# State product of the scan with C as the stationary operand, and the sample's sub-key scores in full-width matmuls

## The chip, the cores and the metric

The kernel runs on one core of a Trainium2 chip. A core has a matrix engine (TensorE, PE in the profile, its weight loads PEld), a vector engine (VectorE, DVE), a scalar engine (ScalarE, ACT), GpSimd (POOL) and SyncE (SP), which only issues transfers; ACT and POOL issue transfers too. Sixteen DMA engines serve them all. Each engine works through its own list of instructions in order and waits for others by semaphores.

The metric is the device time of one launch in microseconds.

## The reference, cut to what matters

One step of a decoder layer for a prompt of 256 tokens and a sample of 8 sequences of 8 tokens each (64 tokens), all in float32, with a model width of 2048: a mixer (a state-space scan, SSD, beside a short convolution), attention over 256 memory tokens, and PEER, which picks 16 experts out of 16384 for each of 8 heads by two sets of 128 sub-keys. The change touches two places. In the scan, for each sequence b, head r of group g and token l:

```python
cb = jnp.einsum('bclgn,bcsgn->bgcls', cc, bc)
y_diag = jnp.einsum('bgcls,bgrcls,bcsgrp->bclgrp', cb, lmat, xdt)
...
y_off = jnp.einsum('bclgn,bcgrpn,bgrcl->bclgrp', cc, new_states[:, :-1], jnp.exp(a_cs))
y = (y_diag + y_off)...
```

For the sample, `new_states[:, :-1]` is the state that comes in from memory (8 sequences, 32 heads, 64 channels a head, 128 state elements). `y_off` is thus, per sequence, the product of 8 rows of C (8 tokens x 128) with the state of each head (64 x 128), scaled by the decay `exp(a_cs)` of head and token. Four groups of 8 heads share one C each.

In PEER the query of a token and head, two halves of 128, is multiplied with the two sets of sub-keys:

```python
q = (xt @ wq).reshape(T, PEER_HEADS, 2, PEER_HALF)
s = jnp.einsum('thid,hikd->thik', q, sub_keys).astype(f32)
s1, i1 = lax.top_k(s[:, :, 0], K)
```

## The kernel before, in words

Activations lie with their 2048 features on 16 blocks of 128 partitions and the 320 tokens along the free axis: columns 0 to 255 are the prompt (`TP` = 256), 256 to 319 the sample (`TS` = 64, `NB` = 8 sequences of `LS` = 8 tokens).

The backbone is a stream of projections. Weights come in tiles W through SyncE's queue into four rooms of half a megabyte (`wtile`). Each half of a tile is split into a high and a low part in a reduced float32 format: ScalarE makes H (line 248), VectorE makes L = W - H (line 249), seven buffers each (`HLB`). TensorE then does three matmuls for each block, of the high and low parts of weight and activation (lines 367 to 369, 320 columns), 12 for a unit of work. The class `Stream` writes the program: weights are loaded `WA` = 3 tiles ahead, splits are made up to `GD` = 6 units ahead of the matmuls, and `pop` emits one unit's matmuls. After each pop, `Stream` advances a list of side generators by a rate each, and these emit everything else: the scan, the attention's softmax, the sub-key scores, the top-16 searches. So the order on TensorE, ScalarE and VectorE is the order in which the program is written; GpSimd's order in these stages is set by a scheduler when the kernel is built. A steady generator also issues, from ScalarE's queue, copies of expert rows from memory to memory (`u_d`), 0.272 of a copy per pop.

The scan (`ssd`, `group`) is a side generator with a rate of 0.7 (`R_SSD`) and runs beside the projections of the scan's inputs and of the short convolution. For each of the four groups g it prepares products of B and C (`ptcb`, line 789 and on), inputs by token (`XD`, `XQ`), and then goes through four chunks j of 128 channels (two heads each). Per chunk: GpSimd has loaded the states of the 8 sequences (`SB`, 128 x 8 x 128, two buffers); TensorE transposes them (`pst`, line 241) and ScalarE copies them to `ST` (line 880), so that the state axis lies on the partitions; then TensorE does the state product `YO` (line 887): for each sequence its `ST` block, 128x128, is stationary and the 8 columns of C are streamed. VectorE multiplies `YO` by the decays `EE` into `YE` (line 888). TensorE forms the new states (`pns`, line 891), VectorE updates `SB` and GpSimd stores it. At the end of a chunk come the within-chunk products `py` (line 913), two heads in two halves of 64 columns of the array, and VectorE adds `py` and then `YE` to `XS` (lines 914 and 915).

In PEER, eight panels of the query projection run through the same stream. `evac_p` multiplies the result by the token norms into q (line 1566, VectorE), two tiles of 128 x 320 a panel. The side generator `scores` multiplies q with the sub-keys `KY`: for the prompt four matmuls (`psc`, line 1578), 128 tokens each; for the sample `pscs` (line 1585), 64 tokens, done twice so that the scores stand on both halves of the 128 partitions. ScalarE copies both to `SS` (lines 1580 and 1586), and VectorE searches them for the top 16 (`best_keys`, lines 1593 to 1601), in the same in-order list as the splits L and the q of later panels. Beside this, `normed` (line 1536 and on) sends the normed input through memory into the tile `XP`.

All matmuls named here other than the projections and pns are in full float32, which the profile records as two passes each.

Of the kernel before, what the change touches and what calls it, by code (L numbers as in the profile page):

```python
# [11 lines left out]
F32 = mybir.dt.float32  # L12
# [151 lines left out]
def step(ctx, tc, ins, outs, dbg=None, stop=None):  # L164
# [417 lines left out]
    strm.then(pMs.close)  # L582


    pS = pSs = DTT = AT = DN = AN = ACN = DD = ACS = EE = BC = REP = DR = MB = None

    def open_s():
        nonlocal pS, pSs, DTT, AT, DN, AN, ACN, DD, ACS, EE, BC, REP, DR, MB
        pS, pSs = pool("pS")
        DTT = pS.tile([NH, T], F32, name="DTT")  # L590
        AT = pS.tile([NH, T], F32, name="AT")
        DN = pS.tile([P, 3, NH], F32, name="DN")
        AN = pS.tile([P, 3, NH], F32, name="AN")
        ACN = pS.tile([P, 3, NH], F32, name="ACN")
        DD = pS.tile([P, 3, NH], F32, name="DD")
        ACS = pS.tile([NH, T], F32, name="ACS")
        EE = pS.tile([P, KC, TS], F32, name="EE")
        BC = pS.tile([P, 8, T], F32, name="BC")

        REP = pS.tile([TS, 2, P], F32, name="REP")  # L600
        S.activation(REP.rearrange("p q (r t) -> p q r t", r=4),
                     ident[0:TS, 0:TS].rearrange("p (q t) -> p q t", q=2).unsqueeze(2).broadcast_to([TS, 2, 4, 32]), AF.Copy)
        DR = pS.tile([P, 2, NH], F32, name="DR")
        MB = pS.tile([P, 4], F32, name="MB")

    strm.then(open_s)

# [138 lines left out]
    def group(g):  # L746
# [42 lines left out]
        PE.matmul(pt[:, 0:TP], Bc[:, 0:P], Cc[:, 0:TP], start=True, stop=True)  # L789
        PE.matmul(pt[:, TP:TP + P], Bc[:, P:TP], Cc[:, P:TP], start=True, stop=True)  # L790
        PE.matmul(pt[0:TS, 384:448], Bc[:, TP:T], Cc[:, TP:T], start=True, stop=True)
        CM = pS.tile([P, 448], F32, tag="CM", bufs=1, name="CM")
        V.tensor_tensor(CM[:, 0:P], pt[:, 0:P], TRI, ALU.mult)
        S.activation(CM[:, P:TP], pt[:, P:TP], AF.Copy)
# [67 lines left out]
            V.tensor_tensor(LM, LM, CM[:, 0:384], ALU.mult)  # L862
            lms.append(LM)

        YE = pS.tile([P, 4, TS], F32, tag="YE", bufs=1, name="YE")
        for j in range(4):
            c = 4 * g + j

# [3 lines left out]
            if j == 0:  # L872
                bcast(1)
            yield 1
            ST = pS.tile([P, NB, P], F32, tag="ST", bufs=1, name="ST")
            for q in range(2):
                pt = ps("pst")
                for b in range(4):
# [3 lines left out]
            yield 1  # L882
            lmat(2 * j + 1)
            yield 1
            YO = ps("YO")
            for b in range(NB):
                PE.matmul(YO[:, LS * b:LS * b + LS], ST[:, b], Cc[:, TP + LS * b:TP + LS * b + LS], start=True, stop=True)
            V.tensor_tensor(YE[:, j], YO[:, 0:TS], EE[:, c], ALU.mult)
            for q in range(2):
                pt = ps("pns")  # L890
                PE.matmul(pt, XQ[:, q, j * P:(j + 1) * P], BD[:, q].rearrange("p b n -> p (b n)"), start=True, stop=True)
# [19 lines left out]
            for pair in zip(*parts):  # L911
                for o, w, m, first, last in pair:
                    PE.matmul(o, w, m, start=first, stop=last)
            V.scalar_tensor_tensor(XS[:, c], XS[:, c], DC[:, c:c + 1], py[:, 0:T], ALU.mult, ALU.add)
            V.tensor_tensor(XS[:, c, TP:T], XS[:, c, TP:T], YE[:, j], ALU.add)
            yield 1

    def mark(*what):
# [643 lines left out]
    def evac_p(m, pt, c):  # L1562
        if m == 0:
            PP["q"] = []
        q = PP["pool"].tile([P, T], F32, tag="q", bufs=2, name="q")
        V.tensor_tensor(q, pt[:, 0:T], RS["p"], ALU.mult)
        PP["q"].append(q)
        if m == 1:
            strm.side(scores(c, PP["q"]), 1)

    def scores(c, qs):
# [9 lines left out]
        yield 1  # L1581
        pt = ps("pscs")
        for j, q in enumerate(qs):
            for r in range(2):
                PE.matmul(pt[TS * r:TS * r + TS, j * P:(j + 1) * P], q[:, TP:T], PP["KY"][:, 2 * c + j], start=True, stop=True)
        S.activation(PP["SS"][:, 2, 2 * c + 1:2 * c + 3], pt[:, 0:2 * P].rearrange("p (j k) -> p j k", k=P), AF.Copy)
        done.add(("score", c))
        yield 1
# [606 lines left out]
```

## Time and profile before

| | before |
|---|---|
| median of 3 runs | 3156.19 us (3151.37 to 3171.6) |
| profiled execution, its own time | 3160.18 us |
| its span, first to last instruction | 3158.5 us |
| TensorE busy | 3091.9 us, 98% |
| weight loads busy | 2829.5 us, 90% |
| VectorE, ScalarE, GpSimd busy | 2277.1, 1597.2, 1306.5 us |
| granted TensorE clock, mean | 0.992 |

The span is what the profile covers; 1.7 us of the profiled execution lie outside it. Busy time of a matmul is from its start to its modelled end, so matmuls that follow each other overlap and the sum of their durations is more than the time they take; the chain of waits shows instead how far each one pushes the next one's start. The scan lies between about 340 and 820 us from the span's start, the sub-key scores between 1530 and 1660. A row of a tile or line has the engine, the operation, what it writes and reads, its count, its shortest, median and longest duration in ns, and the first and last start.

### The profile page before, as it was taken

The numbers are of one execution on the slowest core, as the hardware profiler recorded it, in microseconds if no ns is written. First come the engines' busy times: TensorE is split into PE (matmuls) and PEld (weight loads), VectorE is DVE, ScalarE is ACT, GpSimd is POOL, SyncE is SP. The second block draws the span as 40 slices with busy tenths as digits, with TensorE's granted clock in tenths as the row PEclk, the third lists the DMA queues.
The fourth block names the chain that finished last, engine by engine and source line by source line (L and its number), as shares of the span: only waits on it lengthen the run. The fifth ranks groups of instructions, "written<-read, shape, count | busy, mean of one in ns | idle before, by whom it ended". The sixth has DMA issues, their size and how long they took to land.

```text
span 3158.5 us, 55436 instructions
## 1 busy us (share of the span) xinstructions
PE 3091.9 (98%) x19773; PEld 2829.5 (90%) x19773; DVE 2277.1 (72%) x4498; ACT 1597.2 (51%) x3175; POOL 1306.5 (41%) x1403
## 2 busy tenths in 40 slices
PE   8999999999999999989999999999999999999997
PEld 7889999999999998769999999888888888888886
DVE  5556766666576456556777899888885888888886
ACT  5545544333454344334444444776775555555554
POOL 0011221111100000110239899988887656556553
PEclk9999999999999999999999999999999999999999
DMA  7668899899999999984876788888998999999996
GB/s 262 208 201 294 292 309 309 296 320 300 318 321 312 308 319 240 255 257 154 207 219 211 256 317 318 303 287 305 332 329 269 357 340 350 335 335 325 336 315 195
DMA packets 457955, 909.16 MB, mean 288 GB/s; under 512 B 39584, under 2 KB 269128, under 8 KB 432165
## 3 DMA queue, kind: packets, MB, share of 16 engines
q1 hardware_dynamic: 335564, 562.95, 53.8%
q0 software_dynamic: 54528, 208.44, 19.5%
q10 hardware_dynamic: 67584, 134.23, 12.4%
q8 instruction: 155, 2.54, 0.3%
q14 instruction: 124, 1.01, 0.1%
HBM read 849.41 MB, written 190.05 MB: 329 GB/s over the span
## 4 chain that ended last, share of the span: by engine, by line
PE 75%; DMA 8%; DVE 7%; issue 4%; ACT 3%; POOL 2%; SPq 0%; ACTq 0%; DVEq 0%; POOLq 0%
PE pg L367 9%; PE pg L369 9%; PE pg L368 9%; PE acc L2098 6%; PE acc L2097 6%; PE acc L2096 6%; PE pu L1922 6%; PE pu L1923 3%; PE pu L1929 2%; PE pu L1927 2%; PE pu L1928 2%; DMA W<-in_w_mem_q_dram 2%; PE pg L318 2%; PE pg L319 2%; PE pg L320 2%
## 5 line engine op out<-in xcount | busy, mean ns | idle before, releaser
L249 DVE TENSOR_TENSOR L<-W,H 128x512 fp32r<-128x512 f32 x1320 | 900.5, 710 | 368.6 <-ACT H L248 360.3
L248 ACT ACTIVATE H<-W 128x512 fp32r<-128x512 f32 x1320 | 797.8, 625 | 714.2 <-PE acc L2098 253.8
L1903 POOL TENSOR_TENSOR L<-tt,H 128x512 fp32r<-128x512 f32 x509 | 645.4, 1298 | 73.5 <-ACT H L1900 65.3
L367 PE MATMUL pg<-AH,H 128*128 128x320 f32 (+1 forms) x1872 | 588.7, 314 | 0.0
L369 PE MATMUL pg<-AH,L 128*128 128x320 f32 (+1 forms) x1872 | 579.6, 310 | 0.0
L368 PE MATMUL pg<-AL,H 128*128 128x320 f32 (+1 forms) x1872 | 579.5, 310 | 0.0
L1900 ACT ACTIVATE H<-tt 128x512 fp32r<-128x512 f32 x512 | 311.3, 626 | 183.3 <-DVE tt L1891 146.6
L2097 PE MATMUL acc<-L,wt 128*128 128x512 f32 x1024 | 398.5, 389 | 0.8 <-DVE L L249 0.8
L2096 PE MATMUL acc<-H,wt 128*128 128x512 f32 x1024 | 398.4, 389 | 0.0
L2098 PE MATMUL acc<-H,wt 128*128 128x512 f32 x1024 | 398.3, 389 | 0.0
L1922 PE MATMUL pu<-XP,H 128*128 128x512 f32 x1050 | 377.5, 399 | 2.9 <-ACT g L1835 1.6
L1891 DVE STREAM_TRANSPOSE tt<-W 128x512 f32<-128x512 f32 x512 | 332.9, 687 | 40.5 <-POOL L L1903 32.1
L367 PEld LDWEIGHTS pg<-AH,H 128*128 128x128 f32 (+1 forms) x1872 | 351.5, 188 | 2.8
L368 PEld LDWEIGHTS pg<-AL,H 128*128 128x128 f32 (+1 forms) x1872 | 351.7, 188 | 2.3
L369 PEld LDWEIGHTS pg<-AH,L 128*128 128x128 f32 (+1 forms) x1872 | 351.4, 188 | 0.6
L1923 PE MATMUL pu<-XP,L 128*128 128x256 f32 x1120 | 301.8, 280 | 1.0 <-POOL L L1903 0.8
L1929 PE MATMUL pu<-XP,L 128*128 128x256 f32 x928 | 263.6, 284 | 2.9 <-POOL L L1903 2.8
L2045 POOL TENSOR_TENSOR at<-at,G 128x108 f32<-128x108 f32 x192 | 170.9, 904 | 225.9 <-DMA at<-act_d 193.5
L1927 PE MATMUL pu<-XP,H 128*128 128x256 f32 x928 | 263.2, 284 | 0.0
L1928 PE MATMUL pu<-XP,H 128*128 128x256 f32 x928 | 262.5, 283 | 0.0
L1922 PEld LDWEIGHTS pu<-XP,H 128*128 128x128 f32 x1050 | 197.1, 188 | 44.5 <-ACT g L1835 1.9
L2097 PEld LDWEIGHTS acc<-L,wt 128*128 128x128 f32 x1024 | 192.2, 188 | 41.4 <-DVE L L249 1.3
(488 smaller groups left out, 5807.3 us busy)
## 6 DMA issues: line engine op xcount, KB each, us to landing
u_d<-in_peer_u_dram ACTq DMA_DIRECT2D x128, 1024.0 KB, 8.1
W<-u_d SPq DMA_DIRECT2D x128, 1024.0 KB, 6.4
W<-in_peer_v_dram SPq DMA_DIRECT2D x256, 512.0 KB, 6.5
W<-in_w_in_dram SPq DMA_DIRECT2D x176, 512.0 KB, 7.5
W<-in_w_out_dram SPq DMA_DIRECT2D x64, 512.0 KB, 7.4
W<-in_w_mem_k_dram SPq DMA_DIRECT2D x32, 512.0 KB, 5.2
W<-in_w_mem_v_dram SPq DMA_DIRECT2D x32, 512.0 KB, 4.3
W<-in_w_mem_q_dram SPq DMA_DIRECT2D x32, 512.0 KB, 10.2
```

The lines of the kernel that those rows point to most:

```text
L248: S.activation(h, src, AF.Copy)
L249: V.tensor_tensor(l, src, h.bitcast(F32), ALU.subtract)
L367: PE.matmul(out, hv[:, j, c0:c1], ah[:, k, 0:n], start=st, stop=False)
L368: PE.matmul(out, hv[:, j, c0:c1], al[:, k, 0:n], start=False, stop=False)
L369: PE.matmul(out, lv[:, j, c0:c1], ah[:, k, 0:n], start=False, stop=sp)
L1891: V.transpose(tt.rearrange("p (k a i) -> p k a i", a=4, i=32), box["x", i].rearrange("p (a k j) -> p k a j", a=4, k=16)[:, 4 * q:4 * q + 4])
L1903: G.tensor_tensor(l, src, h.bitcast(F32), ALU.subtract)
L1922: PE.matmul(*wide, start=k == 0, stop=False)
L1923: PE.matmul(pu[:, 0:TP], lv[:, j], PP["xp"][:, 0, k], start=False, stop=False)
L2096: PE.matmul(out, th, h, start=i == 0, stop=False)
L2097: PE.matmul(out, th, l, start=False, stop=False)
L2098: PE.matmul(out, tl, h, start=False, stop=i == P - 1)
```

## The change

In the scan the operands of the state product change places. A new tile `CX` holds, for each sequence, a block of 128 x 32 with the 8 columns of C of that sequence at the place that the sequence has among four, and zeros elsewhere; GpSimd clears it once and ScalarE writes the columns twice a group. For two chunks together, sequence by sequence, `CX` is stationary (32 columns) and the transposed state `ST` of 128 columns is streamed. The four pairs of chunk and half of the sequences go to four groups of 32 output partitions (`YT`), and four matmuls accumulate in each, the zeros keeping the sequences apart. The result has tokens on partitions; ScalarE copies it to `YS`, and one transposition (`YO`) turns it back, behind the products `py` of the second chunk. VectorE's multiply by `EE` and the add to `XS` are done once for both chunks. `ST` gets two buffers instead of one.

In PEER the tile q grows to 384 columns; ScalarE copies the sample's 64 columns behind themselves, and `pscs` becomes one matmul with 128 stationary columns for each q instead of two with 64.

```diff
+        CX = pS.tile([P, NB, 32], F32, name="CX")
+        G.memset(CX, 0.0)
...
+        for q in range(2):
+            to = CX[:, 4 * q:4 * q + 4]
+            S.activation(bass.AP(to.tensor, to.offset, [list(to.ap[0]), [32 + LS, 4], [1, LS]]),
+                         Cc[:, TP + 32 * q:TP + 32 * q + 32].rearrange("p (b l) -> p b l", l=LS), AF.Copy)
...
-        YE = pS.tile([P, 4, TS], F32, tag="YE", bufs=1, name="YE")
+        YE = pS.tile([P, 2, TS], F32, tag="YE", bufs=1, name="YE")
+        sts = []
...
-            ST = pS.tile([P, NB, P], F32, tag="ST", bufs=1, name="ST")
+            ST = pS.tile([P, NB, P], F32, tag="ST", bufs=2, name="ST")
+            sts.append(ST)
...
-            YO = ps("YO")
-            for b in range(NB):
-                PE.matmul(YO[:, LS * b:LS * b + LS], ST[:, b], Cc[:, TP + LS * b:TP + LS * b + LS], start=True, stop=True)
-            V.tensor_tensor(YE[:, j], YO[:, 0:TS], EE[:, c], ALU.mult)
+            if j % 2:
+                YT = ps("YT")
+                for b in range(4):
+                    for o in range(2):
+                        for q in range(2):
+                            r = 64 * o + 32 * q
+                            PE.matmul(YT[r:r + 32, 0:P], CX[:, 4 * q + b], sts[j - 1 + o][:, 4 * q + b],
+                                      start=b == 0, stop=b == 3)
+                YS = pS.tile([P, P], F32, tag="YS", bufs=1, name="YS")
+                S.activation(YS, YT[:, 0:P], AF.Copy)
...
+            if j % 2:
+                YO = ps("YO")
+                transpose(YO[:, 0:P], YS)
             V.scalar_tensor_tensor(XS[:, c], XS[:, c], DC[:, c:c + 1], py[:, 0:T], ALU.mult, ALU.add)
-            V.tensor_tensor(XS[:, c, TP:T], XS[:, c, TP:T], YE[:, j], ALU.add)
+            if j % 2:
+                pair = slice(c - 1, c + 1)
+                V.tensor_tensor(YE, YO[:, 0:P].rearrange("p (c t) -> p c t", t=TS), EE[:, pair], ALU.mult)
+                V.tensor_tensor(XS[:, pair, TP:T], XS[:, pair, TP:T], YE, ALU.add)
...
-        q = PP["pool"].tile([P, T], F32, tag="q", bufs=2, name="q")
-        V.tensor_tensor(q, pt[:, 0:T], RS["p"], ALU.mult)
+        q = PP["pool"].tile([P, TP + P], F32, tag="q", bufs=2, name="q")
+        V.tensor_tensor(q[:, 0:T], pt[:, 0:T], RS["p"], ALU.mult)
+        S.activation(q[:, T:T + TS], q[:, TP:T], AF.Copy)
...
-            for r in range(2):
-                PE.matmul(pt[TS * r:TS * r + TS, j * P:(j + 1) * P], q[:, TP:T], PP["KY"][:, 2 * c + j], start=True, stop=True)
+            PE.matmul(pt[:, j * P:(j + 1) * P], q[:, TP:TP + P], PP["KY"][:, 2 * c + j], start=True, stop=True)
```

What stands where, on TensorE, in the second chunk of the first group, at the state product. First before (pg is a projection, its number a buffer; each row gives the output, the operands and the shape):

```order
L368 MATMUL pg_3699<-AL,H 128x320
L369 MATMUL pg_3699<-AH,L 128x320
L887 MATMUL YO<-BC,ST 128x8 x8
L891 MATMUL pns<-BD,XQ 128x512
L367 MATMUL pg_3698<-AH,H 128x320
```

And the same place after the change:

```order
L368 MATMUL pg_3693<-AL,H 128x320
L369 MATMUL pg_3693<-AH,L 128x320
L899 MATMUL YT<-ST,CX 32x128 x16
L905 MATMUL pns<-BD,XQ 128x512
L367 MATMUL pg_3692<-AH,H 128x320
```

Eight matmuls became sixteen of another shape, at the same place; in the first chunk the row of YO is gone and nothing stands for it. At the end of the same chunk, on TensorE, after the change:

```order
L368 MATMUL pg_3924<-AL,H 128x320
L369 MATMUL pg_3924<-AH,L 128x320
L927 MATMUL py<-LM,XD 64x128 x6
L927 MATMUL py<-MS,XD 64x64 x2
L241 MATMUL YO<-ident,YS 128x128
L367 MATMUL pg_3923<-AH,H 128x320
L368 MATMUL pg_3923<-AL,H 128x320
```

The transposition is new; before, the projection followed py at once. On ScalarE, in the score stage, around the second panel's q, before (xh is the normed input on its way to XP):

```order
L248 ACTIVATE xh<-xn 128x256
L1586 ACTIVATE SS<-pscs 128x256
L248 ACTIVATE H<-W 128x512 x3
L248 ACTIVATE xh<-xn 128x256
L248 ACTIVATE H<-W 128x512
```

And after the change:

```order
L248 ACTIVATE xh<-xn 128x256
L1606 ACTIVATE SS<-pscs 128x256
L248 ACTIVATE H<-W 128x512 x2
L1587 ACTIVATE q<-q 128x64 x2
L248 ACTIVATE H<-W 128x512
L248 ACTIVATE xh<-xn 128x256
```

Two copies now stand between the second split and the third one, and each of them waits for VectorE's q.

More of the change, by code (lines that the diff above doesn't have):

```diff
@@ L582, in step @@
     strm.then(pMs.close)
-    pS = pSs = DTT = AT = DN = AN = ACN = DD = ACS = EE = BC = REP = DR = MB = None
+    pS = pSs = DTT = AT = DN = AN = ACN = DD = ACS = EE = BC = REP = DR = MB = CX = None
     def open_s():
-        nonlocal pS, pSs, DTT, AT, DN, AN, ACN, DD, ACS, EE, BC, REP, DR, MB
+        nonlocal pS, pSs, DTT, AT, DN, AN, ACN, DD, ACS, EE, BC, REP, DR, MB, CX
         pS, pSs = pool("pS")
```

## The prediction

> **What bounds the kernel now.** I read the page's head first, then the table of busy time by stage, then the chain of waits in the two stages that the change touches, and last the waits there.
>
> ```profile
> span 3158.5 us, 55436 instructions
> PE 3091.9 (98%) x19773; PEld 2829.5 (90%) x19773; DVE 2277.1 (72%) x4498; ACT 1597.2 (51%) x3175; POOL 1306.5 (41%) x1403
> ```
>
> TensorE is busy for 98% of the span, so the question is how much of its time goes. The stages, from the state-space scan (340 to 820 us) on, then the output projections, the attention and the PEER query with its sub-key scores (1530 to 1660 us):
>
> ```profile
> core 0: us, PE busy (x) PEld busy (x) DVE busy (x) ACT busy (x) POOL busy (x), PEclk, DMA share, GB/s
> 340.00:820.00 480.00, 479.33 (x3488) 468.76 (x3487) 316.04 (x709) 204.48 (x382) 79.43 (x179) 1.00 0.90 303
> 820.00:1180.00 360.00, 357.72 (x2443) 355.55 (x2442) 206.63 (x367) 173.57 (x319) 16.64 (x31) 1.00 0.94 320
> 1180.00:1400.00 220.00, 199.39 (x1745) 172.35 (x1744) 124.09 (x217) 83.23 (x190) 25.54 (x36) 0.95 1.01 252
> ...
> 1530.00:1660.00 130.00, 127.83 (x936) 124.52 (x936) 101.95 (x399) 56.50 (x114) 49.44 (x78) 0.99 0.80 221
> ```
>
> In the scan TensorE stands still for 0.7 of 480 us, in the score stage for 2.2 of 130. Both are TensorE-bound, though the DMA engines are 0.90 busy in the first. VectorE (316 of 480 us) and ScalarE (204 of 480) have room. What TensorE loses here in work should leave the end time, unless transfers or another engine come late instead.
>
> **The change on TensorE: the scan.** The state product YO, as the trace has it:
>
> ```profile
> L887 PEld LDWEIGHTS YO<-BC,ST x256: 186/192/192, 351.0 to 794.8; 128*128 128x128 f32 x128
> L887 PE MATMUL YO<-BC,ST x256: 170/256/277, 351.0 to 794.9; 128*128 128x8 f32 x128
> L888 DVE TENSOR_TENSOR YE<-YO,EE x16: 216/224/225, 356.3 to 795.2; 128x64 f32<-128x64 f32 x16
> ```
>
> There are 16 visits (one YE each) of 8 matmuls, each matmul recorded as two passes, so 16 passes a visit. A pass loads 128x128 weights to stream 8 columns. These durations overlap in the pipeline; what a visit takes from the stream is read off the chain of waits, first around one visit in the second group, then at the very first one:
>
> ```profile
> 474.82 0.87 PE pst L241 x8
> ...
> 480.98 1.68 PE YO L887 x16
> 482.66 0.33 PE pns L891
> ...
> 485.19 0.23 PE pns L891
> ...
> 499.86 1.68 PE YO L887 x16
> ...
> 507.82 1.07 PE py L913 x16
> ```
>
> ```profile
> 351.02 1.95 PE YO L887 x16
> ```
>
> A visit takes 1.68 us, and the pns behind it is 0.10 longer than the pns that follows ordinary work (0.33 against 0.23). That is 1.78 us, 16 times 28.5 us; the first visit is 0.27 longer. Removed: 28.8 us.
>
> In its place come 8 visits of 16 matmuls (YT), with 32 stationary columns and 128 moving ones, going round four column groups. The trace of before has the same form elsewhere: the attention scores of the sample (pss), 128x32 stationary, 128 moving, f32, four column groups in turn, 8 matmuls a visit.
>
> ```profile
> 1264.12 0.15 PE pg L1131
> 1264.27 0.57 PE pss L1348 x16
> 1264.85 0.34 PE pg L1129
> ```
>
> The visit takes 0.57 us and the projection matmul behind it 0.34 instead of 0.15: 0.76 us for 8 matmuls. What a full-width matmul of 128 moving columns costs stands in the chain of the score stage, where psc is 4 of them and pscs 4 half-width ones:
>
> ```profile
> 1593.28 0.89 PE psc L1578 x8
> 1594.17 0.14 PE pg L367
> ...
> 1595.93 0.59 PE pscs L1585 x8
> 1596.52 0.34 PE pg L367
> ```
>
> So 0.22 us each (0.89/4), with no loss behind. Eight at a quarter of that are 0.44 us, which leaves 0.32 us of fixed cost in a pss visit. YT has 16 matmuls: 16 x 0.22/4 + 0.32 = 1.20 us. Its ends are 0.88 (no fixed cost) and 2 x 0.76 = 1.52 (twice a pss visit); I take 1.20, the same row with its fixed part counted once.
>
> [...] The trace gives pss 1.76/0.76 = 2.3x, so I stay with the row. [...]
>
> The transposition of the pair is one pass: pst does 8 in 0.87 us, so 0.11. [...] A pair of chunks thus costs 1.31 us instead of 3.56: 2.25 less, 8 times 18.0, and 18.3 with the long first visit.
>
> **The score stage.** pscs now is two full-width matmuls. Before: 0.59 + (0.34 - 0.14) = 0.79 us. After: 2 x 0.22 = 0.44 (0.45 by the unrounded row). Eight panels: 2.8 us less. Together TensorE loses 21.1 us, between 18.5 (YT at 1.52) and 23.7 (YT at 0.88).
>
> **What the other engines get.** ScalarE has the nearest rows in the scan and in the score stage:
>
> ```profile
> L708 ACT ACTIVATE XS<-cv,CB 128x64 f32<-128x64 f32 x10 | 3.3, 334 | 0.0
> ```
>
> ```profile
> L1586 ACT ACTIVATE SS<-pscs 128x256 f32<-128x256 f32 x8 | 3.0, 375 | 0.0
> ```
>
> The 8 copies into CX and 16 into q (at most 0.33 each) and 8 copies YS (at most 0.38) come to 11 us, spread over 610 us in which ScalarE is idle for more than half. VectorE has 16 small multiplies and 16 adds of 0.22 us fewer and 8 of each at double width, at most 0.45 each: never more than before. GpSimd clears CX once, ahead of the scan. None of that is on TensorE's path by its length. By its waits it could be:
>
> - YS is needed by the transposition, which stands behind py, while YT stands where the odd chunk's YO stood. From the YO at 499.86 to the py at 507.82 are 8.0 us. A copy of 0.4 us hides there even behind several splits of a weight.
> - YE was a wait of VectorE in the middle of a chunk; it goes. The new YE waits for the transposition, right behind an update that waits for py anyway:
>
> ```profile
> ACT H L248 <- PE pg L368: 106.6, 75, 3.2
> ...
> POOL SB L761 <- DMA out_dram<-SB: 98.6, 14, 8.7
> ...
> DVE YE L888 <- PE YO L887: 13.0, 12, 1.8
> ...
> ACT H L248 <- DMA W<-in_w_in_dram: 8.5, 6, 3.0
> ```
>
> Those 13.0 us never held TensorE, so nothing is gained from them.
> - The copy of YS makes ScalarE wait for YT, with the next splits queued behind. But ScalarE already spends 106.6 us waiting for TensorE to give a split buffer back: it is as far ahead as the buffers let it be, and the copy stops it at about the point where it would stop anyway. I cost it at nothing.
> - What is late next would be the weights: W held a split up for 8.5 us in all, 3.0 at most, and TensorE never noticed, since up to seven split units lie ahead, of 12 matmuls of 0.15 us or 1.8 us each. The scan gets 18.3 us shorter of 480, 4%, and the DMA share goes from 0.90 to about 0.94, which the next stage already runs at with 2.3 us of idle TensorE. Nothing for this in the sum.
> - GpSimd issues a few reads of XP and copies of XNS in another order. The last read was issued at 1602.23, the first matmul on XP ran at 1642.1, so there are 40 us to spare. Nothing:
>
> ```profile
> 1602.23 0.59 POOL L1547 DMA_DIRECT2D XP<-xl_d  x1
> ```
>
> ```profile
> L1927 PE MATMUL pu<-XP,H x928: 278/283/386, 1642.1 to 1984.2; 128*128 128x256 f32 x186
> ```
>
> **The rivals.** *The gain is handed back to the transfers.* From 820 to 1400 us the DMA share is 0.94 and then 1.01, and between 1180 and 1400 TensorE loses 20.6 us to waits. If the copies issued in the scan pile up, part of the 21 us is waited for there. For it: those shares. Against it: they are issued as units are worked off, so they move with TensorE, and the scan leaves 48 of its 480 us of DMA time idle. Half handed back is 3156 - 10.5 = 3146 us.
>
> *The column groups do not overlap.* If every 32-column load had to wait for the matmul before it, a visit would cost its loads:
>
> ```profile
> L1348 PEld LDWEIGHTS pss<-tt,qm x512: 106/110/178, 1207.6 to 1370.3; 128*32 128x32 f32 x171
> ```
>
> 32 loads of 0.11 are 3.52 us, with 0.32 fixed and 0.11 for the transposition 3.95 a pair: 0.39 more than before, 8 times 3.1 us, less 2.8 from pscs and 0.3: 3156 us, no change. Against it: a pss visit has 16 such loads, 1.76 us on end, and takes 0.57. [...]
>
> *Slower: the copies into q stop ScalarE behind VectorE.* Each is queued between splits and waits for VectorE's q, which stands behind long runs of top-16 searches. TensorE has waited for q once, and what followed shows what a standstill costs:
>
> ```profile
> PE psc L1578 <- DVE q L1566: 2.2, 1, 2.2
> ```
>
> ```profile
> DVE L L249 <- ACT H L248: 11.9, 12, 4.8
> ```
>
> ```profile
> 1544.23 1.16 PE psc L1578 x8
> 1545.78 0.27 PE pg L369
> ...
> 1548.45 0.80 PE pscs L1585 x8
> ```
>
> Behind the 2.2 us the projection matmuls took 0.27 instead of 0.15 for ten rows, and psc and pscs 0.27 and 0.21 more than in later panels: 1.7 us. Splits delayed by ScalarE's 4.8 us, the longest that VectorE waited for one here, would cost 4.8 + 1.7 = 6.5 us a panel if nothing lay ahead; eight panels are 52 us, less 21: 3187 us, 1% slower. It decides only once the delay exceeds the split units in stock, 6 of 1.8 us, some 11 us; 4.8 is less than half of that.
>
> **How the numbers follow.** The profiled execution took 3160.18 us, 4.0 above the median of the runs; 21.1 less is 3139.1, and against the median of 3156.19 it is 3135. About 1% (31.6 us) is what a measurement of this kernel can tell from no change, and 21.1 us are 0.67%.
>
> - Forecast, nearly all of the 21 us arrives: 0.68.
> - Part handed back, about 3146: 0.14.
> - No overlap, 3156: 0.04.
> - ScalarE stops, up to 3187: 0.07.
> - More than the sum, by standstills that vanish too: 0.07. Behind the first YO the chain has twelve projection matmuls at 0.27 (first and last below), 1.5 us, and the runs of before reach 4.8 us below their median (3151.37): 3156 - 23.7 - 1.5 - 4.8 = 3126.
>
> ```profile
> 354.35 0.27 PE pg L368
> ...
> 357.28 0.27 PE pg L367
> ```
>
> The range is 3123 to 3158: its low end is this last case with a little room, its high end full give-back with the few us by which medians differ. Faster by over 1% needs 10 us beyond TensorE's whole loss: 0.06. Slower by over 1% is the upper half of the ScalarE case and what I have not thought of: 0.05. Within 1%: 0.89.
>
> **What would show it.** In the changed profile the chain should have YT x32 at about 1.2 us (0.9 to 1.5) in the scan, eight times, with pns at about 0.33 behind; one transposition of 0.11 behind every second py; pscs x4 at 0.45 with 0.15 behind. The scan's start-to-end should shrink by 18 us and the score stage by 3, with TensorE still busy all through, and the DMA share at 0.93 to 0.95. YT near 3.5 us would be the second rival. Waits of TensorE for YS, W or H in the scan, or idle TensorE between 820 and 1400 us growing past 23 us, would be the first. Waits of TensorE for splits between 1510 and 1640 us would be the third. The forecast is wrong if the time leaves 3123 to 3158, and wrong in its reason if YT's visits and the end time do not move together.

## The result and the profile after

The changed kernel takes 3137.15 us (median of 6 runs, 3130.6 to 3147.57); the kernel before, run beside it, 3155.57 us (median of 6). The ratio is 0.9943, with a 95% interval of 0.9925 to 0.9961: 18 us less, between 12 and 24. The prediction said 3135 us and 21 us less, and took about 1% as the least that can be told from no change; six runs of each kernel make 0.6% clear, though not whether it is 18 us or 21. The profiled execution took 3135.79 us.

The head of the page after; the columns are busy time, its share of the span, and instructions:

```profile
span 3134.1 us, 55394 instructions
PE 3069.0 (98%) x19749; PEld 2808.1 (90%) x19749; DVE 2274.6 (73%) x4482; ACT 1602.5 (51%) x3207; POOL 1292.1 (41%) x1404
```

TensorE is still the bound, with 22.9 us less of busy time in a span that is 24.4 us shorter. The same table by stage, with the same columns, as before the change; from 820 us on, a window now covers work that lies some 20 us later in the program:

```profile
340.00:820.00 480.00, 477.94 (x3622) 464.10 (x3622) 318.99 (x707) 211.68 (x409) 82.99 (x186) 1.00 0.93 316
...
1180.00:1400.00 220.00, 199.59 (x1756) 169.88 (x1755) 124.33 (x206) 83.75 (x191) 27.67 (x40) 0.96 0.99 256
...
1530.00:1660.00 130.00, 125.68 (x942) 124.72 (x942) 107.86 (x446) 61.19 (x126) 59.70 (x73) 1.00 0.74 217
```

The 2.1 us that TensorE lacks in the first window are nearly all one wait for a transfer at 819 us, behind the scan, which stood in the next window before the change. The DMA share of the scan rose from 0.90 to 0.93, and between 1180 and 1400 us TensorE is idle for 20.4 us, as it was for 20.6. Cut by the program instead, from the last store of the scan's result to the last add of the attention's output, it is idle for 22 us, and was for 24.

Now the new operations. One visit of the state product in the first group, in the order of TensorE's starts (start, duration, operation):

```profile
368.84 0.31 PE L369 MATMUL pg<-AH,L 128*128 128x320 f32 x1
369.08 1.08 PE L899 MATMUL YT<-ST,CX 128*32 128x128 f32 x32
370.09 0.50 PE L905 MATMUL pns<-BD,XQ 128*128 128x512 f32 x1
370.43 0.31 PE L367 MATMUL pg<-AH,H 128*128 128x320 f32 x1
```

From the start of the projection ahead of it to the start of the one behind it are 1.59 us. Of these 0.15 are the projection's own turn and 0.24 those of pns, which leaves 1.20 us for YT, with the 0.10 by which this pns takes longer (0.34 us from its start to that of the projection behind). (Durations overlap: the projections last 0.31 us and start 0.15 apart. So all visits below are measured from start to start like this.) The transposition, at the end of the same chunk, with the projection ahead of py and the second one behind it:

```profile
375.79 0.31 PE L369 MATMUL pg<-AH,L 128*128 128x320 f32 x1
...
377.10 0.33 PE L241 MATMUL YO<-ident,YS 128*128 128x128 f32 x1
...
377.41 0.30 PE L368 MATMUL pg<-AL,H 128*128 128x320 f32 x1
```

The stretch from the projection ahead of py to the second one behind it lasts 1.62 us here and 1.56 in the chunks that have no transposition (mean of eight each 1.626 and 1.560). The transposition costs 0.07 us. A pair of chunks thus pays 1.27 us for the state product instead of 3.56.

And the chain of waits at one pscs:

```profile
1572.79 0.44 PE pscs L1605 x4
1573.23 0.15 PE pg L367
```

pscs takes 0.44 us, and the projection behind it has its ordinary 0.15: no loss.

How long the scan lasts can be read from two groups of instructions, the first transposition of a state (pst) and the last store of the scan's result (ysc_d). After the change:

```profile
L241 PE MATMUL pst<-ident,SB x128: 270/272/273, 344.4 to 768.0; 128*128 128x128 f32 x128
L992 POOL DMA_DIRECT2D ysc_d<-ysc x16: 540/568/610, 456.0 to 809.7; - x16
```

From 344.4 to 809.7 are 465.3 us. Before, in the profile on which the prediction rests:

```profile
L241 PE MATMUL pst<-ident,SB x128: 270/272/273, 344.1 to 787.9; 128*128 128x128 f32 x128
L972 POOL DMA_DIRECT2D ysc_d<-ysc x16: 543/569/667, 462.7 to 830.5; - x16
```

486.4 us, that is 21.1 more. Behind the scan the gap between the two executions grows little: the last store is 20.8 us earlier, the first wide matmul of PEER's output stage 21.9, the end 24.4. So most of the gain is made in the scan and is kept; whether the score stage has a part in it is one of the questions below.

### The profile page after: what moved, and what is told of

It is laid out like the page before. It is cut to its first block, busy times and chain, and to the rows that moved or that the text cites. A ratio compares the mean times of both kernels' runs of the same rounds, so it can differ in the third digit from the quotient of the medians.

```text
span 3134.1 us, 55394 instructions
## 1 busy us (share of the span) xinstructions
PE 3069.0 (98%) x19749; PEld 2808.1 (90%) x19749; DVE 2274.6 (73%) x4482; ACT 1602.5 (51%) x3207; POOL 1292.1 (41%) x1404
## 5 line engine op out<-in xcount | busy, mean ns | idle before, releaser
L2065 POOL TENSOR_TENSOR at<-at,G 128x108 f32<-128x108 f32 x192 | 157.9, 836 | 241.4 <-DMA at<-act_d 184.0
```

## The experiments

The theory after the result: TensorE's time in the scan becomes time of the kernel one to one; it gained 18 us there by YT's visits, and nothing in the score stage, where the freed time is waited away. The rivals: part of the scan's gain comes from waits or from VectorE rather than from TensorE; part of it is handed back to transfers; the score stage gives its 2.8 us. And within YT: what sets its 1.20 us, the loads of the 32 columns, the streamed columns, or the order of the groups.

The kernels ran in three sets, each beside its own runs of the kernel before (medians 3153.8, 3155.93 and 3157.25 us). "Scan" below is the stretch from the first pst to the last store ysc_d, read from the same two groups as above.

### The scan's part alone

The score stage as before, the scan as changed:

```diff
-        q = PP["pool"].tile([P, TP + P], F32, tag="q", bufs=2, name="q")
-        V.tensor_tensor(q[:, 0:T], pt[:, 0:T], RS["p"], ALU.mult)
-        S.activation(q[:, T:T + TS], q[:, TP:T], AF.Copy)
+        q = PP["pool"].tile([P, T], F32, tag="q", bufs=2, name="q")
+        V.tensor_tensor(q, pt[:, 0:T], RS["p"], ALU.mult)
...
-            PE.matmul(pt[:, j * P:(j + 1) * P], q[:, TP:TP + P], PP["KY"][:, 2 * c + j], start=True, stop=True)
+            for r in range(2):
+                PE.matmul(pt[TS * r:TS * r + TS, j * P:(j + 1) * P], q[:, TP:T], PP["KY"][:, 2 * c + j], start=True, stop=True)
```

> Only the scan is changed; q and pscs are as before. My theory (the gain is the time that TensorE no longer spends on the state product, and it arrives whole): from the first pst to the last store of ysc the scan is about 20.5 us shorter than before, as in the changed kernel; from the first psc to the last psc the score stage stays at 114.4 us; the median is 17 to 21 us under the kernel before. Rival (the two parts only work together, or part of the gain is in the score stage): the scan shrinks by less than 15 us.

Measured: 3141.02 us, ratio 0.9957 (0.9939 to 0.9975), 8 to 19 us less than before. The scan lasts 465.8 us, 17.6 to 20.6 less than in the two profiles of before. By the medians the end gains 12.8 us, less than the 17 to 21 expected: in the profile the output stage behind takes 4.3 us more than in the changed kernel, with the same code. The interval holds both 17 and 13, so the scan's part alone carries the gain as far as the timing can tell.

### The score stage's part alone

The reverse: the scan of the kernel before, with q of 384 columns, its copy, and pscs in full-width matmuls.

> Only q and pscs are changed; the scan is as before. My theory: the scan takes the time of before; from the first psc to the last psc 114.4 us become about 111.6 to 112, a pscs of four passes takes 0.45 us with nothing behind; the end moves by -3 us at most, too little for the timing to tell. Rival (the chain of copies x2s_d behind it sets the start of PEER): the first matmul pu comes no earlier than before relative to the first psc, 110.7 us after it, and the part is worth nothing. Rival that ends slower (the copies into q stop ScalarE): TensorE waits for H or L in the stage, and it gets longer than 114.4 us. If the clock drop behind the first YO belongs to that YO, it is here again.

Measured: 3156.26 us, ratio 1.0008 (0.9995 to 1.0021): between 2 us less and 7 more. The 2.8 us that the prediction gave this part lie just outside. Its trace says why. TensorE's waits from the last add of the attention's output (XN) to the first wide matmul of the output stage (each row: who waited for what, total us, times, longest), first here:

```profile
PE psc L1579 <- DVE q L1566: 3.8, 3, 2.1
PE pu L1929 <- POOL L L1903: 3.6, 5, 1.8
PE pxn L241 <- ACT xx L1650: 1.5, 1, 1.5
```

then in the kernel before:

```profile
PE pu L1929 <- POOL L L1903: 2.8, 4, 1.8
PE psc L1578 <- DVE q L1566: 2.2, 1, 2.2
```

TensorE does less and waits 8.9 us instead of 5.0 (4.8 in the second profile of before, below). A new wait has come, for the doubled copy xx of the normed sample by ScalarE, which the transpositions pxn behind the last panel need. The whole change shows the same, 7.3 us (6.3 in its second profile):

```profile
PE psc L1599 <- DVE q L1586: 3.0, 3, 2.1
PE pu L1949 <- POOL L L1923: 2.4, 3, 1.8
PE pxn L241 <- ACT xx L1670: 1.9, 1, 1.9
```

And the stretch itself does not get shorter. The last XN and the first wide pu, before and after, and the narrow form of pu (256 columns) that comes first, after:

```profile
L1071 DVE TENSOR_TENSOR XN<-XN,pg x16: 478/482/489, 1420.7 to 1507.5; 128x320 f32<-128x320 f32 x16
...
L1922 PE MATMUL pu<-XP,H x1050: 387/395/503, 1984.8 to 2440.2; 128*128 128x512 f32 x175
```

```profile
L1091 DVE TENSOR_TENSOR XN<-XN,pg x16: 479/484/489, 1398.9 to 1485.7; 128x320 f32<-128x320 f32 x16
...
L1942 PE MATMUL pu<-XP,H x1050: 389/394/505, 1962.9 to 2416.4; 128*128 128x512 f32 x175
...
L1947 PE MATMUL pu<-XP,H x928: 277/283/416, 1617.9 to 1962.3; 128*128 128x256 f32 x186
```

477.3 us before, 477.2 after; with the score stage's part alone it is 478.3, with the scan's alone 477.5. Up to the first narrow pu a gain is there: 132.2 us from the last XN after (132.9 in the second profile, 133.0 with this part alone), against 134.6 before (134.0 in the second profile, 134.3 with the scan's part alone). It is lost behind that. ScalarE starts on xx 142.2 us behind the last XN before and after alike (141.7 to 142.6 in these six executions), so TensorE comes to pxn earlier and waits there.

### The state product five times over

If TensorE's time counts one to one, more of it must cost what less of it gained.

```diff
+                for _ in range(5):
+                    for b in range(4):
+                        for o in range(2):
+                            for q in range(2):
...
```

> The changed kernel with the 16 matmuls of each YT visit done five times over (same result). My theory: a visit takes 80 x 0.055 + 0.32 = 4.7 us instead of 1.2, so 8 visits add 28 us, and all of it arrives: the median is about 28 us above the changed kernel, some 9 us above the kernel before. Rival (transfers hide or take up a part of TensorE's time in the scan): clearly less than 28 us at the end, with TensorE's waits falling.

Measured: 3172.62 us, ratio 1.0067 (1.0047 to 1.0087): by the medians 18.8 us more than before, where the change has 18.4 less, 37 between them. The scan lasts 494.2 us, 28.9 more than with one product. One visit:

```profile
369.69 0.31 PE L369 MATMUL pg<-AH,L 128*128 128x320 f32 x1
369.93 4.58 PE L900 MATMUL YT<-ST,CX 128*32 128x128 f32 x160
374.44 0.50 PE L906 MATMUL pns<-BD,XQ 128*128 128x512 f32 x1
374.77 0.31 PE L367 MATMUL pg<-AH,H 128*128 128x320 f32 x1
```

5.08 - 0.39 = 4.69 us. Four products more are thus 3.49 us, 0.87 each, and 1.20 - 0.87 leaves a fixed 0.33 a visit: the split of 0.88 and 0.32 that the prediction had borrowed from pss. Eight visits of 3.49 are 27.9 us, and the scan grew by 28.9; one of the eight is 1.3 us longer than the others, with an idle 0.9 us inside it. The end follows less closely: the span is 37.3 us longer than with one product. Between the scan and the last XN 6.4 us less are taken than in the changed kernel, and in the output stage (from the first wide pu on) 14.2 more, with the same code in both places.

### No state product at all

YT, YS, the transposition YO, YE and its add are taken out.

```diff
-            if j % 2:
-                YT = ps("YT")
...
-                YS = pS.tile([P, P], F32, tag="YS", bufs=1, name="YS")
-                S.activation(YS, YT[:, 0:P], AF.Copy)
...
-                YO = ps("YO")
-                transpose(YO[:, 0:P], YS)
...
-                V.tensor_tensor(YE, YO[:, 0:P].rearrange("p (c t) -> p c t", t=TS), EE[:, pair], ALU.mult)
-                V.tensor_tensor(XS[:, pair, TP:T], XS[:, pair, TP:T], YE, ALU.add)
```

> The changed kernel without the state product: YT, YS, the transposition YO, YE and its addition to XS are left out, so the part of y that comes from the incoming state is missing. My theory: TensorE loses a further 8 x (1.2 + 0.06) = 10 us and all of it arrives: about 10 us under the changed kernel, 28 under the kernel before, and the scan some 30 us shorter than before. Rival (the DMA engines are the next bound and take the gain back): the scan shrinks by clearly less, TensorE waits for W, H or L between 340 and 860 us, and the end stays near the changed kernel's.

Measured: 3131.92 us, ratio 0.993 (0.9911 to 0.9948): 21.9 us under the kernel before, not 28.

```profile
L241 PE MATMUL pst<-ident,SB x128: 270/272/301, 344.2 to 759.5; 128*128 128x128 f32 x128
L975 POOL DMA_DIRECT2D ysc_d<-ysc x16: 543/568/610, 453.9 to 799.7; - x16
```

The scan lasts 455.5 us, 9.8 less than with the product. Eight times 1.27, what YT and the transposition take of TensorE, are 10.2. So what the product still costs is TensorE's time; neither ScalarE's copies, VectorE's multiplies nor the wait for YS has a price that the scan shows. The time of the whole kernel shows only part of it: by the medians it is 3.5 us more than the change gains. The output stage, with identical code, is where the executions of different kernels differ too: in its last accumulations TensorE waits 3.8 us here, 7.5 with five products and 3.1 with the scan's part alone, for low parts L of weights that come late, against 0.8 before and nothing in the change. Nothing in the scan was seen to lead to that.

### The groups one after the other

The same sixteen matmuls of YT, each group's four together instead of going round.

```diff
-                for b in range(4):
-                    for o in range(2):
-                        for q in range(2):
+                for o in range(2):
+                    for q in range(2):
+                        for b in range(4):
```

> The changed kernel with the 16 matmuls of a YT visit in another order: all four of one column group, then all four of the next, instead of going round the groups. My theory (a visit is short because matmuls in different column groups run beside each other): the order takes that away, a visit takes up to 16 x 0.22 + 0.32 = 3.8 us, the scan is 8 x 2.6 = 21 us longer than in the changed kernel, no better than before. Rival (32 stationary columns cost a quarter of the time in any order): a visit stays at 1.2 us.

Measured: 3145.03 us (one run), and this visit:

```profile
368.24 0.31 PE L369 MATMUL pg<-AH,L 128*128 128x320 f32 x1
368.48 2.46 PE L899 MATMUL YT<-ST,CX 128*32 128x128 f32 x32
370.87 0.51 PE L905 MATMUL pns<-BD,XQ 128*128 128x512 f32 x1
371.21 0.31 PE L367 MATMUL pg<-AH,H 128*128 128x320 f32 x1
```

2.97 - 0.39 = 2.58 us. Neither of the two expected values. Less the fixed 0.32, if that part is the same in this order, it is 2.26/32 = 0.071 us a pass, where a full-width one takes 0.11. The scan lasts 476.7 us, 11.4 more than with the change; eight visits of 1.38 more are 11.0.

### Two groups at a time

Going round two groups, then round the other two.

```diff
-                for b in range(4):
-                    for o in range(2):
+                for o in range(2):
+                    for b in range(4):
                         for q in range(2):
```

> The changed kernel with YT's matmuls going to and fro between two column groups, then between the other two. New theory (load 0.027 us, and a pass in one group takes 0.074 with its stream, as measured with the groups in turn; two groups overlap): 0.037 us a pass, 32 x 0.037 + 0.32 = 1.5 us a visit. Rival (any change of group is enough to hide the stream whole): 1.2 us. Rival (what costs is the accumulation into the same columns): also 1.2.

Measured: 3149.38 us (one run), scan 468.4 us.

```profile
366.35 0.31 PE L369 MATMUL pg<-AH,L 128*128 128x320 f32 x1
366.59 1.54 PE L899 MATMUL YT<-ST,CX 128*32 128x128 f32 x32
368.06 0.50 PE L905 MATMUL pns<-BD,XQ 128*128 128x512 f32 x1
368.40 0.31 PE L367 MATMUL pg<-AH,H 128*128 128x320 f32 x1
```

2.05 - 0.39 = 1.66 us, or 0.042 a pass: more than the theory's 1.5, and clearly not the 1.2 of both rivals. With more groups in turn a pass took less: 0.071 us with one, 0.042 with two, 0.0275 (0.88/32) with four.

### Half the streamed columns

Each matmul of YT streams 64 of the 128 columns of the state; the loads stay as they are, 32 a visit. (Half of the state product is left out, and the copy YS becomes two of 64 columns.)

```diff
-                            PE.matmul(YT[r:r + 32, 0:P], CX[:, 4 * q + b], sts[j - 1 + o][:, 4 * q + b],
+                            PE.matmul(YT[r:r + 32, 0:64], CX[:, 4 * q + b], sts[j - 1 + o][:, 4 * q + b, 0:64],
```

> The changed kernel with 64 instead of 128 columns of the state streamed in each matmul of YT; the other half of the product is left out (the first half's result stands in its place). New theory (a pass costs the load of its stationary columns, 32 of them 0.027 us, as long as the columns it streams go to another group than the one before): a visit stays at 1.2 us. The prediction's own picture (a full-width pass of 128 streamed columns, shared by four groups): the part that grows with the stream is halved, 0.88 to 0.44, a visit takes 0.76 us.

Measured: 3133.89 us (one run), scan 460.7 us.

```profile
366.77 0.31 PE L369 MATMUL pg<-AH,L 128*128 128x320 f32 x1
367.01 0.65 PE L899 MATMUL YT<-ST,CX 128*32 128x64 f32 x32
367.59 0.50 PE L906 MATMUL pns<-BD,XQ 128*128 128x512 f32 x1
367.93 0.31 PE L367 MATMUL pg<-AH,H 128*128 128x320 f32 x1
```

1.16 - 0.39 = 0.77 us: the part above the fixed 0.32 has halved, from 0.88 to 0.45, as the prediction's own picture had it. So with four groups in turn and the same 32 loads, that part went with the streamed columns; the theory of 0.027 us a load is out.

### Before and after once more

The kernel before and the changed kernel again, each with a profile, for what differs between executions of one kernel.

> The kernel before once more, for a second profile of it: what a stage differs by here between two executions of one program is what a difference between two kernels has to exceed. If the wait of 0.65 us and the fall of the clock at the first YO are chance, they need not be here; the scan then takes about 2.5 us less than in the first profile.

Measured: 3153.07 us (one run), and a scan of 483.4 us:

```profile
L241 PE MATMUL pst<-ident,SB x128: 270/272/273, 342.5 to 784.4; 128*128 128x128 f32 x128
L972 POOL DMA_DIRECT2D ysc_d<-ysc x16: 542/570/612, 459.2 to 825.9; - x16
```

That is 3.0 us less than in the first profile of before, and the same as with the score stage's part alone, whose scan is that of before (483.3). In the first profile TensorE waited 0.6 us for ST ahead of the first YO and then had twelve projection matmuls at 0.27; here it waited 0.3, and the projections behind it start every 0.15 us. The first YO itself takes 1.95 us in both, and again with the score stage's part alone. So 3 of the 21 us by which the two first profiles differ in the scan come and go between executions of one kernel; the change itself is worth 18.

> The changed kernel once more, for a second profile of it: the scan as in the first, shorter than the first profile of before by 20 to 22 us and than the second by about 18.

Measured: 3133.78 us (one run), a scan of 464.9 us, 18.5 less than in the repeated before. Of the 19.4 us between the spans of these two (3151.4 and 3132.0), 18.5 are made in the scan.

### What makes TensorE wait in the score stage

Three runs tried to get the 2.8 us. First, the buffer xs, through which ScalarE hands the normed input to the store into memory: two of half the size. In the changed kernel ScalarE waits 4.1 us for one such store (x2s_d), 3.4 in the kernel before, and xx comes behind it.

```diff
-                if q % 2 == 0:
-                    xs = pp.tile([P, 1024], F32, tag="xs", bufs=1, name="xs")[0:n]
+                xs = pp.tile([P, 512], F32, tag="xs", bufs=2, name="xs")[0:n]
```

> The changed kernel with the tile xs, through which the input of PEER goes to memory, as two tiles of 512 columns with a transfer each, in place of one of 1024 with a transfer for two copies. Theory (the 2.8 us of the score stage are lost because ScalarE waits for the transfer x2s_d before it makes xx, which the transposition pxn needs): ScalarE's wait for x2s_d, 4.1 us, goes, TensorE's wait for xx, 1.9 us, goes with it, and from the first psc to the last pxn it takes 123 us instead of 124.9. Rival (the search for the top 16 on VectorE sets that end): no change, 124.9. At the end of the kernel at most 2 us, which the timing cannot tell.

Measured: 3138.53 us, ratio 0.9943 (0.992 to 0.9965), that of the whole change. ScalarE's wait for x2s_d is gone, but at the same copy it now waits 4.5 us for TensorE, and xx starts 143.0 us behind the last XN, no earlier than the 142.2 of the changed kernel. TensorE still waits 3.3 us for q and 1.1 for xx; from the first psc to the last pxn are 125.8 us instead of 124.9, and the stretch from XN to the wide pu is 477.6 us. That wait alone was not the cause. It can become one: in the run with two groups at a time ScalarE waited 6.4 us for the same store, TensorE then 5.1 us for xx, and the stretch was 483.2 us.

Second, the copy of q by VectorE in place of ScalarE, which then has no wait for q:

```diff
-        S.activation(q[:, T:T + TS], q[:, TP:T], AF.Copy)
+        V.tensor_tensor(q[:, T:T + TS], pt[:, TP:T], RS["p"][:, TP:T], ALU.mult)
```

> The changed kernel with the second copy of the sample's columns of q made by VectorE, as a product from the same source, instead of ScalarE. Theory (ScalarE's waits for q, 20 us in all, cost TensorE something in this stage): TensorE's waits for q and xx, 4.9 us in the changed kernel, fall to the 2.2 us of before. Rival (those waits of ScalarE are covered): they stay between 4 and 6 us.

Measured: 3137.35 us (one run). ScalarE's waits for q, in the changed kernel

```profile
ACT q L1587 <- DVE q L1586: 21.3, 9, 4.8
```

are gone, and TensorE waits 2.5 us for q and 0.9 for xx, 3.4 instead of 4.9 (or 4.0 in the repeated run). The stretch is 477.5 us. So those 21.3 us, 4.8 at most as the third rival had it, cost TensorE about a microsecond, and the kernel nothing that can be seen.

Third, the matmuls that wait are placed later: psc and the transpositions pxn each come four pops behind their operands instead of two.

```diff
         yield from until("ky")
-        yield from wait(2)
+        yield from wait(4)
...
-        yield from wait(2)
+        yield from wait(4)
         for q in range(4):
             pt = ps("pxn")
```

> The changed kernel with psc two units later behind its q, and pxn two units later behind xx. Theory (the score stage does not get shorter because TensorE arrives at psc and pxn before VectorE and ScalarE have made what it reads, and their lists, not their busy time, are the reason): TensorE's waits there, 4.9 us, go to under 1, and from the first psc to the last pxn it takes 122 to 124 us instead of 124.9 plus the two to four units, 3.5 to 7 us, by which pxn itself moves; the first matmul behind PEER's change of stage comes 2 to 3 us earlier. Rival (VectorE sets the pace of the stage as a whole): the waits come back at another place, as waits for H, L or tt, and nothing is gained.

Measured: 3144.5 us, ratio 0.9969 (0.9955 to 0.9984). TensorE's waits for q fell to 0.4 us and those for xx to nothing, and the first narrow pu comes 129.5 us behind the last XN, 2.7 earlier than in the changed kernel, much as the theory had it. But behind it waits have come in their place, as the rival had it:

```profile
PE pu L1949 <- POOL L L1923: 4.1, 5, 1.8
PE pu L1947 <- ACT H L1920: 3.4, 2, 2.3
```

The first is 2.4 in the changed kernel, the second is not there. The first wide pu comes 486.4 us behind the last XN, 9 later than in the changed kernel:

```profile
L1091 DVE TENSOR_TENSOR XN<-XN,pg x16: 478/481/489, 1385.5 to 1472.4; 128x320 f32<-128x320 f32 x16
...
L1942 PE MATMUL pu<-XP,H x1035: 387/395/795, 1958.8 to 2410.0; 128*128 128x512 f32 x173
```

Not all of that is loss: the kernel does four more units in the narrow form (944 matmuls of each of its three lines instead of 928) before it changes to the wide one, and four fewer in the wide one; at the changed kernel's pace, 344.4 us for 928, they are 5.9 us. Less these, the stretch is 480.5 us. The waits for q and xx were not the only bound of this stretch, then: without them it is not shorter. What else is, the runs do not settle. VectorE is the candidate, busy in the changed kernel for 176.5 of the last 185 us before the wide form (176.6 before):

```profile
1778.00:1963.00 185.00, 182.60 (x1502) 181.74 (x1500) 176.50 (x428) 87.71 (x162) 172.50 (x142) 0.99 0.86 314
```

but no run took work from VectorE there alone, and GpSimd is at 172.5 us.

## Why the prediction was right, point by point

**TensorE's time in the scan counts one to one: right, for the length of the scan.** Seven kernels put it to the test. If the scan is the 455.5 us of the kernel without a state product, plus eight times the visit and 0.07 for the transposition, it comes out like this; the row of before is 16 visits of 1.78 us, without a transposition:

| state product | a visit, us | scan by the sum | scan measured |
|---|---|---|---|
| half the columns | 0.77 | 462.2 | 460.7 |
| the change | 1.20 | 465.7 | 465.3, 464.9 |
| two groups at a time | 1.66 | 469.3 | 468.4 |
| groups one after the other | 2.58 | 476.7 | 476.7 |
| before | 1.78 x 2 | 484.0 | 483.4 (486.4 in the first profile) |
| five times over | 4.69 | 493.6 | 494.2 |

All but the first profile of before lie within 1.5 us of the sum, over a spread of 33. For the end of the kernel the change shows it (18.5 of 19.4 us between the second profiles); five products and none do not follow one to one there.

**YT's visit, 1.20 us: right in size, 1.20 measured,** and with it the 18.3 us of the scan (18.1 to 18.5 against the repeated before). The step was "sixteen matmuls at a quarter of a full-width one, and a fixed 0.32". The fixed part is confirmed by the fivefold product (0.33). The quarter holds as a number (0.88/32 is a quarter of 0.11), but not because four groups run four times as fast: in the order one group after the other a pass already costs 0.071 us instead of 0.11, and going round the four makes it 0.0275, 2.6 times less. The prediction assumed the quarter without knowing of these two factors; that they multiply to four was luck. Of the 2.29 us that a pair of chunks gained, 3.56 - (2.58 + 0.07) = 0.91 are the change of operands with the groups one after the other, and 1.38 the order of the loops.

**The transposition: over by a little,** 0.07 us instead of 0.11, 0.3 us in all. **The long first visit: right.** The first YO takes 1.95 us in the repeated before too, and the first YT no longer than the others, so these 0.3 us are the change's. The slow projections behind the first YO are not: only the first profile has them.

**The score stage, 2.8 us: the step that failed.** pscs fell from 0.79 to 0.44 us as worked out, but the step behind it, that this stage is TensorE-bound because TensorE lacks only 2.2 of its 130 us, did not hold. Of the 2.8 us, 1.3 to 2.4 still stand between the first and the last psc (114.4 and 114.0 us in the two executions of before, 112.0 and 112.7 after); the wait of pxn for xx, which comes no earlier than before, then takes 1.6 to 1.9, and by the wide pu nothing is left. What fixes the time of xx stays open. That this part alone gives a ratio of 1.0008 agrees. The sum should have been 18, and the measured median difference is 18.

**The rivals.** Handed back to transfers: no. The DMA share went to 0.93, as forecast, and the idle time of the later window stayed (20.4 and 20.6 us). No overlap of the column groups: no, at 1.20 us instead of nearly 4. With the stream halved, a visit of 0.77 us even holds the same 32 loads, which the changed kernel's profile records at 0.11 each, 3.5 us on end:

```profile
L899 PEld LDWEIGHTS YT<-ST,CX x256: 105/110/111, 369.1 to 774.1; 128*32 128x32 f32 x128
```

ScalarE behind VectorE: the waits came as large as named (4.8 us at most, a number that the prediction had from another wait), and TensorE waited for no split between 1510 and 1640 us, which fits the 11 us of delay that the prediction asked for. What came in place of it was smaller and at another spot, xx. More than the sum: no. A standstill of 0.6 us and its slow projections vanished between the two profiles, but the repeated before has 0.3 us of the one and nothing of the other, so the slow stretch was not the old kernel's to lose.

## What to carry to other kernels

A stage in which TensorE idles for 2% (2.2 of 130 us here) can still refuse what TensorE saves: of the 0.35 us saved eight times nothing was left by the first wide pu, and 1.6 to 1.9 us went into the wait for xx. So ask how soon the next operand comes. Where a small product loads much and streams little, as YO did with 128x128 loaded for 8 columns, it is worth trying to let the large operand stream and the small one stand, split over column groups, and to go round the groups matmul by matmul: here a pair of chunks went from 3.56 us to 1.27, transposition included, while the same matmuls group by group took 2.58 a visit instead of 1.20. Before a gain of a few microseconds is read from two profiles, a second profile of the unchanged kernel tells how much of it is chance: the scan of before took 486.4 us in one and 483.4 in the other.

## What the runs showed of the hardware

The float32 passes of psc and YO, with 128 stationary columns, took 0.11 us, though psc streams 128 columns (0.89/8) and YO 8 (1.78/16). Those of YT, with 32 stationary columns and 128 streamed, took (less the fixed 0.32 a visit) 0.071 when their neighbours went to the same group, 0.042 with two groups in turn, 0.0275 with four, and 0.014 with four and 64 streamed. Whether the 128 stationary columns are what holds a pass at 0.11 was not shown: no run changed the stationary columns alone. And four groups side by side did not run at four times the pace of one, but at 2.6 (0.071/0.0275).

Slow matmuls stood behind some short standstills and not behind others. Behind the 2.0 us for which TensorE waits for xr in the changed kernel, the granted clock is 0.66 over the 5 us from 818 us on, and the projections between 820.10 and 822.24 start 0.27 us apart instead of 0.15:

```profile
819.02 1.01 PE L241 MATMUL pt<-ident,xr 128*128 128x128 f32 x4 [2.04 <-DMA xr<-in_x_prompt_dram]
819.69 0.61 PE L367 MATMUL pg<-AH,H 128*128 128x320 f32 x1
```

```profile
818.00:823.00 5.00, 3.98 (x18) 4.01 (x19) 2.77 (x5) 3.48 (x6) 0.54 (x1) 0.66 1.04 396
```

In the first profile of before, the same wait, 2.3 us long, left no such trace (its projections start every 0.15 us, and the granted clock from 836 to 845 us is 1.00), while 0.6 us ahead of the first YO did: the slow projections behind that start between 354.35 and 357.28, with a granted clock of 0.50 from 354.3 to 357.6. Those twelve projections lost 1.5 us, more than the standstill itself. Both stretches last some 3.2 us (819.69 to 822.9 in the changed kernel). Why the one standstill had such a stretch behind it and the other had not, no run tested.
